# Fox/RetNet trunk on one core: ScalarE's reads of a transposed tile issued ahead of VectorE's

## The chip, the cores and the metric

The kernel runs on one core of a Trainium2 chip. The metric is the device time of one execution in microseconds (us). Five engines work side by side, each through its own instructions in the order in which they were issued: TensorE (PE in the profile; its weight loads are PEld), VectorE (DVE), ScalarE (ACT), GpSimd (POOL, here used to issue DMAs) and SyncE (SP, which issues the other DMAs). They wait for each other through semaphores.

## The reference

Two layers over x (1, 512, 2048), each with its own token mixer, and a LayerNorm behind each.

```python
def reference(x, ...):
    h = x
    for i in range(2):
        y = fox_branch(...) if i % 2 == 0 else retention_branch(...)
        h = layer_norm(DEEPNORM_ALPHA * h + y, ln_gain[i], ln_bias[i])
    return h

def fox_branch(x, w_in, b_f, q_gain, k_gain, w_out):     # 16 heads of 128
    q, k, v, gate, f_logit = split(x @ w_in)
    q = rms_norm(heads(q), q_gain)                       # over each head's 128
    k = rms_norm(heads(k), k_gain)
    c = cumsum(log_sigmoid(f_logit + b_f))
    s = q @ k.T * 128 ** -0.5 + c[:, None] - c[None, :]  # causal
    o = softmax(s) @ v
    return (o * silu(gate)) @ w_out

def layer_norm(x, g, b):
    return (x - mean(x)) * rsqrt(var(x) + 1e-5) * g + b
```

The second layer (`retention_branch`) projects the first layer's output into queries, keys, values and gates of 8 heads, applies a rotary turn, a decaying causal product, a group norm, the gate and an output projection.

## The kernel before, in words

**Products in three parts.** Every fp32 operand is split into a high part (`h`, rounded to the matmul's format; a ScalarE copy, L325) and a low part (`l` = value minus `h`; a VectorE subtraction, L326). `mm3` makes one product of three matmuls (L330 to L332). For a block of weights the parts are `w_h` and `w_l`, in rings of three buffers, of 128 x 1024 elements each.

**Blocks in a fixed order.** The projections are cut into blocks of weights of 512 KB: `w_raw` and `w_q` are the loaded weights, `acc` the accumulators in PSUM. Many units use a scheme of seven products instead of eight, whose weights are sums (VectorE, L595) and whose activations are sums too (forms "a" and "s"). A block of the wide kind is 12 matmuls of 512 columns.

**A planner at build time.** The class `Order` writes down, slot by slot, the order in which each engine gets its work. A slot splits the weights of the block two ahead, multiplies one block, and then lets the waiting tasks take one step each. Tasks are Python generators; each `yield need(...)` names what the step costs by the planner's own estimate, and which buffers it takes. The planner changes nothing at run time: the engines go through what was written. The order between engines is then put in as waits by the tile framework, which looks at what each instruction reads and writes, in the order in which the program issues them.

**Two small PSUM buffers.** `mmp` is a ring of two buffers of 128 x 512 fp32, one PSUM bank each. Transposes, scores and other small products go through them, between the blocks.

**Queries and keys of the first layer.** For each of 8 pairs of heads, the task `Pair.normed` scales the raw queries and keys (L1093), and for each of four pieces of 128 positions transposes them on TensorE into an `mmp` buffer `t`: columns 0 and 1 are the two heads' queries, 2 and 3 their keys. `to_parts` then reads `t` and writes the high part to the tile `qk_h` (ScalarE, L1102, with the gain as scale) and the low part to the tile `qk_l` (VectorE, L1103, which reads `t` and the high part), first for the queries and then for the keys. That makes 32 calls, and 64 instructions on each engine. In pairs 6 and 7 (`quick`, transposes at L1112; others at L1122) the four pieces follow each other closely. The scores in `head` read `qk_h` and `qk_l`.

**The first layer's end.** The task `to_columns(m)` normalises 256 rows `z` and turns them into columns, the second layer's input. In 8 turns per `m` it transposes four 128 x 128 pieces of `z` into an `mmp` buffer (L1567); one turn later, four instructions read that buffer, multiply by the gain and add the bias, each for one column `j`, into the tile `raw` (named `aq` in the program): VectorE takes `j == 1` (L1583), ScalarE the other three (L1585). That is 16 instructions on VectorE and 48 on ScalarE. With `m == 0`, one turn later, `split_form` splits the piece into high and low part (`a`, L325 and L326). Between the turns the blocks' own splits (`w_h`, `w_l`) go through the same two engines.

Of the kernel before, what the change touches and what calls it, by code (L numbers as in the profile page):

```python
# [14 lines left out]
AF = mybir.ActivationFunctionType  # L15
ALU = mybir.AluOpType

P = 128
# [227 lines left out]
def need(dve=0.0, act=0.0, pe=0.0, wait=1, until=lambda: True, **rings):  # L246
    return dict(dve=dve, act=act, pe=pe, wait=wait, until=until, rings=rings)
# [3 lines left out]
def trunk(ctx: ExitStack, tc: tile.TileContext, xq, x, fb_f, columns, wf_in, narrow, wide, ln_g, ln_b, rot, decay,  # L251
          out):
    nc = tc.nc
# [7 lines left out]
    def f32(t):  # L261
        return t.bitcast(F32)
# [34 lines left out]
    gq, gk = cols[:, 0:1], cols[:, 1:2]  # L297
# [6 lines left out]
    def rsqrt_steps(dst, src, n, scale, eps, steps=True):  # L304

        h = pool.tile([P, n], F32, name="rsq_h", tag=f"rsq_h{n}")
        t = pool.tile([P, n], F32, name="rsq_t", tag=f"rsq_t{n}")

        nc.vector.tensor_scalar(h, src, 0.5 * scale, 0.5 * eps, op0=ALU.mult, op1=ALU.add)
        nc.vector.tensor_scalar(t.bitcast(I32), h.bitcast(I32), 1, None, op0=ALU.logical_shift_right)  # L310
        nc.vector.tensor_scalar(dst.bitcast(I32), t.bitcast(I32), -1.0, float(0x5EF759DF - 2 ** 31),
                                op0=ALU.mult, op1=ALU.add)
        for i in range(3):
            if i == 1 and steps:
                yield need(dve=1.2, wait=0)
            if n == 1:
                nc.vector.scalar_tensor_tensor(t, dst, h, dst, op0=ALU.mult, op1=ALU.mult)
            else:
                nc.vector.tensor_mul(t, dst, dst)
                nc.vector.tensor_mul(t, t, h)  # L320
            nc.vector.scalar_tensor_tensor(dst, t, 1.5, dst, op0=ALU.subtract, op1=ALU.mult)
# [670 lines left out]
    class Pair:  # L992
# [88 lines left out]
        def normed(self):  # L1081

            yield need(until=lambda: self.have == 4 and fox["norms"] == self.i)
            raw = [self.raw[s // 2][:, s % 2] for s in range(ST)]
            r = self.ss
            yield need(dve=1.2)
            yield from rsqrt_steps(*[r.rearrange("p a b -> p (a b)")] * 2, 4 * ST, 1.0 / P, QK_EPS)
            scaled = {}
            for s in range(ST):
                yield need(dve=0.6, wait=0)  # L1090
                scaled[s] = o.due
                v = raw[s].rearrange("p (h d) -> p h d", h=4)
                nc.vector.tensor_mul(v, v, r[:, s, :, None].to_broadcast([P, 4, P]))  # L1093
            yield need(until=lambda: all(free[t] for t in self.tags))
            for t in self.tags:
                take(t)
            self.qk = sb8("qk_h", self.tags[0], F32R), sb8("qk_l", self.tags[1], F32R)

            def to_parts(t, s):
                for i, gain in ((0, gq), (2, gk)):  # L1100
                    h, l = (p[:, i:i + 2, s * P:(s + 1) * P] for p in self.qk)
                    nc.scalar.activation(h, t[:, i:i + 2], AF.Copy, scale=gain)  # L1102
                    nc.vector.scalar_tensor_tensor(l, t[:, i:i + 2], gain, f32(h), op0=ALU.mult, op1=ALU.subtract)  # L1103
                self.due = o.due
                give("mmp")

            t, s, last = {}, ST if self.quick else 0, None
            for q in range(ST if self.quick else 0):
                yield need(act=0.75, dve=0.7, pe=0.45, wait=1 - q % 2, mmp=1, until=lambda: o.soon(scaled[q]))
                t[q] = by4(mmp())  # L1110
                for h in range(4):
                    nc.tensor.transpose(t[q][:, h], raw[q][:, h * P:(h + 1) * P], ident)  # L1112
                to_parts(t[q], q)
            can = lambda: s < ST and free["mmp"] and o.soon(scaled[s])
            while s < ST or last is not None:
                yield need(act=0.75, dve=0.7, pe=0.45, until=lambda: last is not None or can())
                new = None
                if can():
                    new = s
                    t[s] = by4(mmp())  # L1120
                    for h in range(4):
                        nc.tensor.transpose(t[s][:, h], raw[s][:, h * P:(h + 1) * P], ident)  # L1122
                    s += 1
                if last is not None:
                    to_parts(t[last], last)
                last = new
            give("in0")
            give("in1")
            fox["emptied"] = self.i + 1
            yield need()  # L1130
            fox["norms"] = self.i + 1
# [396 lines left out]
    def to_columns(m):  # L1528
        yield need(dve=2.6, until=lambda: quarters[2 * m] == quarters[2 * m + 1] == 4)
        quarters[2 * m] = quarters[2 * m + 1] = 0  # L1530
        mv, r = ln_factors(2 * m, 2 * m + 1)
        nb = pool.tile([P, 2], F32, name="ln_nb", tag="ln_nb", bufs=2)
        nc.vector.scalar_tensor_tensor(nb, mv[:, :, 0], -1.0, r, op0=ALU.mult, op1=ALU.mult)
        due = {}
        for e in range(2):
            yield need(dve=0.81, act=0.97)
            due[2 * m + e] = o.due
            for u in range(2):
                s = 2 * m + e
                z = z_part(s, u)  # L1540
                if u:
                    nc.scalar.activation(z, z, AF.Identity, scale=r[:, e:e + 1], bias=nb[:, e:e + 1])
                else:
                    nc.vector.tensor_scalar(z, z, mv[:, e, 0:1], r[:, e:e + 1], op0=ALU.subtract, op1=ALU.mult)
                nc.gpsimd.dma_start(z_norm[s][:, u * 1024:(u + 1) * 1024], z)
        if m == 0:
            new_quarters(0)
            new_form("a11")
            new_form("a12")
        else:  # L1550
            yield need(g0=1, g2=1)
            new_quarters(1)

        turns = [(2 * m + e, c) for c in ((0, 1, 2, 3) if m == 0 else (0, 2, 1, 3)) for e in range(2)]
        ps, i, last, made = {}, 0, None, []
        can = lambda: i < 8 and free["mmp"] and o.soon(due[turns[i][0]])
        while i < 8 or last is not None or made:
            yield need(dve=(0 if last is None else 0.35) + 0.6 * len(made), act=(0 if last is None else 0.9) + 0.5 * len(made),
                       pe=0.45, until=lambda: last is not None or made or can())
            new = None  # L1560
            if can():
                new = i
                s, c = turns[i]
                zs = z_part(s, c // 2)[:, c % 2 * 512:(c % 2 + 1) * 512]
                ps[i] = by4(mmp())
                for j in range(4):
                    nc.tensor.transpose(ps[i][:, j], zs[:, j * P:(j + 1) * P], ident)  # L1567
                i += 1
            for j in made:
                s, c = turns[j]  # L1570
                es = slice(s % 2 * P, (s % 2 + 1) * P)
                k = c % 2 * 4
                split_form(f"a1{c // 2 + 1}", aq[f"1{c // 2 + 1}"][:, k:k + 4, es], k, k + 4, es, s % 2 == 1)
            made = []
            if last is not None:
                s, c = turns[last]
                es = slice(s % 2 * P, (s % 2 + 1) * P)
                d = aq[f"{m + 1}{c // 2 + 1}"][:, c % 2 * 4:c % 2 * 4 + 4, es]
                for j in range(4):
                    k = c * 4 + j  # L1580
                    g, b = cols[:, 2 + k:3 + k], cols[:, 2 + KT + k:3 + KT + k]
                    if j == 1:
                        nc.vector.tensor_scalar(d[:, j], ps[last][:, j], g, b, op0=ALU.mult, op1=ALU.add)  # L1583
                    else:
                        nc.scalar.activation(d[:, j], ps[last][:, j], AF.Identity, scale=g, bias=b)  # L1585
                give("mmp")
                if m == 0:
                    made.append(last)
                elif s % 2:
                    there.add((f"2{c // 2 + 1}", c % 2))  # L1590
            last = new
        for u in range(2):
            for t in z_tags(u, m):
                give(t, 2)
            for key in ((u, m), (u, 2 * m), (u, 2 * m + 1)) if (u, m) == (1, 1) else ((u, m),):
                zt.pop(key, None)
# [435 lines left out]
```

## Time and profile before

| | |
|---|---|
| median of 3 runs | 2371.23 us (2368.53 to 2372.38) |
| profiled execution, own time | 2373.73 us |
| its span, first to last instruction | 2372.0 us |
| mean granted TensorE clock | 0.993 |
| busy: PE, DVE, ACT, POOL | 97%, 80%, 51%, 7% |
| high parts L1102 on ScalarE | 64 of 469 ns mean, first at 144.0, last at 798.1 us |
| low parts L1103 on VectorE | 64 of 481 ns mean, first at 146.5, last at 798.6 us |
| columns L1585 on ScalarE | 48 of 452 ns mean, first at 936.2, last at 1022.0 us |
| columns L1583 on VectorE | 16 of 405 ns mean, first at 937.4, last at 1021.2 us |

How to read the profile's lines: a row of the timeline gives start, length, engine, line, operation, `out<-in`, and in brackets the idle time of the engine just before it and what ended that. "x2" merges neighbours. Rows of waits give who waited for whom. In the table of windows each engine's busy time in that stretch is followed by the granted clock (1.00 is full speed) and the share of the DMA engines.

### The profile page before, as it was taken

What the parts mean: (1) busy time and instruction counts of PE and PEld (TensorE: products, weight loads), DVE (VectorE), ACT (ScalarE), POOL (GpSimd) and SP (SyncE); (2) the same over time, 40 slices, a digit from 0 to 9 for tenths busy, and PEclk for the clock granted to TensorE, in tenths of its full rate; (3) what the DMA queues carried; (4) which work ended last, traced back from release to release, by engine and by line L of the source; (5) the groups of instructions that cost most, each with busy time, mean ns of one, the idle gap of its engine ahead of it and who ended that gap; (6) DMA issues with size and microseconds to landing.
All of it is one profiled execution on the core that took longest, in us unless ns stands there. A gap on an engine that the chain in (4) does not pass through costs nothing.

```text
span 2372.0 us, 32919 instructions
## 1 busy us (share of the span) xinstructions
PE 2307.9 (97%) x12424; PEld 1975.0 (83%) x12424; DVE 1892.5 (80%) x2477; ACT 1213.4 (51%) x1762; POOL 165.7 (7%) x256
## 2 busy tenths in 40 slices
PE   9999999999999999999999999999999999999995
PEld 9878778879899778888889898988888898787784
DVE  5887787787765656689889888888988889987877
ACT  4546556556555534565444545354545445554533
POOL 0000000000000000010100101010101000011002
PEclk9999999999999999999999999999999999999998
DMA  6356455455544456684685857575756659679778
GB/s 225 123 199 198 160 187 187 154 181 184 195 151 155 139 199 241 225 186 157 207 263 211 249 174 222 197 203 186 218 186 209 204 171 274 209 256 295 234 247 190
DMA packets 186350, 477.36 MB, mean 201 GB/s; under 512 B 18224, under 2 KB 63424, under 8 KB 185680
## 3 DMA queue, kind: packets, MB, share of 16 engines
q1 hardware_dynamic: 160288, 399.48, 50.3%
q0 software_dynamic: 25904, 75.78, 12.7%
q8 instruction: 97, 1.59, 0.3%
q14 instruction: 61, 0.50, 0.1%
HBM read 415.39 MB, written 64.00 MB: 202 GB/s over the span
## 4 chain that ended last, share of the span: by engine, by line
PE 62%; DVE 7%; DMA 4%; issue 3%; ACT 3%; POOL 0%; SPq 0%; DVEq 0%; ACTq 0%; POOLq 0%
PE acc L330 19%; PE acc L331 19%; PE acc L332 19%; DVE w_l L326 3%; DMA w_raw<-in_wide 2%; ACT w_h L325 2%; PE mmp L331 1%; PE mmp L330 1%; PE mmp L332 1%; PE mmp L1303 1%; DVE w_q L595 1%; DMA room<-in_wide 1%; PE mmp L1835 1%; PE mmp L1155 0%; DVE z L1936 0%
## 5 line engine op out<-in xcount | busy, mean ns | idle before, releaser
L325 ACT ACTIVATE w_h<-w_q 128x1024 fp32r<-128x1024 f32 x360 | 380.6, 1059 | 417.9 <-DVE w_q L595 221.6
L326 DVE TENSOR_TENSOR w_l<-w_raw,w_h 128x1024 fp32r<-128x1024 f32 x314 | 383.5, 1222 | 201.8 <-ACT w_h L325 200.5
L330 PE MATMUL acc<-w_h,a 128*128 128x512 f32 (+1 forms) x1440 | 536.5, 373 | 7.2 <-DVE kept L488 4.6
L331 PE MATMUL acc<-w_l,a 128*128 128x512 f32 (+1 forms) x1440 | 529.4, 368 | 3.1 <-DVE w_l L326 2.9
L332 PE MATMUL acc<-w_h,a 128*128 128x512 f32 (+1 forms) x1440 | 528.9, 367 | 0.0
L325 ACT ACTIVATE w_h<-w_raw 128x1024 fp32r<-128x1024 f32 x314 | 331.7, 1058 | 374.5 <-PE acc L332 181.0
L326 DVE TENSOR_TENSOR w_l<-w_q,w_h 128x1024 fp32r<-128x1024 f32 x360 | 439.2, 1221 | 100.3 <-ACT w_h L325 96.7
L331 PE MATMUL acc<-w_l,s 128*128 128x512 f32 (+1 forms) x1280 | 488.4, 382 | 10.7 <-DVE w_l L326 10.7
L330 PE MATMUL acc<-w_h,s 128*128 128x512 f32 (+1 forms) x1280 | 492.2, 385 | 1.6 <-ACT w_h L325 1.6
L332 PE MATMUL acc<-w_h,s 128*128 128x512 f32 (+1 forms) x1280 | 486.9, 380 | 0.0
L330 PEld LDWEIGHTS acc<-w_h,a 128*128 128x128 f32 x1440 | 272.5, 189 | 54.1 <-issue 8.5
L331 PEld LDWEIGHTS acc<-w_l,a 128*128 128x128 f32 x1440 | 272.8, 189 | 48.6 <-DVE w_l L326 7.5
L332 PEld LDWEIGHTS acc<-w_h,a 128*128 128x128 f32 x1440 | 272.3, 189 | 45.2
L331 PEld LDWEIGHTS acc<-w_l,s 128*128 128x128 f32 x1280 | 241.9, 189 | 60.0 <-DVE w_l L326 17.6
L332 PEld LDWEIGHTS acc<-w_h,s 128*128 128x128 f32 x1280 | 241.6, 189 | 45.8
L330 PEld LDWEIGHTS acc<-w_h,s 128*128 128x128 f32 x1280 | 241.6, 189 | 45.0 <-ACT w_h L325 2.0
L595 DVE TENSOR_TENSOR w_q<-w_q,w_raw 128x1024 f32<-128x1024 f32 x216 | 263.3, 1220 | 12.1 <-DMA w_raw<-in_wide 9.7
L332 PE MATMUL acc<-a,w_l 128*128 128x256 f32 x464 | 132.2, 285 | 1.7 <-DVE w_l L326 1.7
L330 PE MATMUL acc<-a,w_h 128*128 128x256 f32 x464 | 132.3, 285 | 1.5 <-ACT w_h L325 1.5
L331 PE MATMUL acc<-a,w_h 128*128 128x256 f32 x464 | 132.0, 285 | 0.0
L332 PE MATMUL acc<-s,w_l 128*128 128x256 f32 x448 | 126.8, 283 | 0.0
L331 PE MATMUL acc<-s,w_h 128*128 128x256 f32 x448 | 126.7, 283 | 0.0
(235 smaller groups left out, 2972.2 us busy)
## 6 DMA issues: line engine op xcount, KB each, us to landing
w_raw<-in_wide SPq DMA_DIRECT2D x364, 512.0 KB, 4.1
w_raw<-in_narrow SPq DMA_DIRECT2D x104, 512.0 KB, 3.7
w_q<-in_wide SPq DMA_DIRECT2D x72, 512.0 KB, 4.4
room<-in_wide SPq DMA_DIRECT2D x48, 512.0 KB, 4.5
y_s<-ny POOLq DMA_DIRECT2D x48, 256.0 KB, 7.1
y_s<-y POOLq DMA_DIRECT2D x40, 256.0 KB, 6.7
w_q<-in_narrow SPq DMA_DIRECT2D x18, 512.0 KB, 3.9
room<-in_narrow SPq DMA_DIRECT2D x18, 512.0 KB, 3.9
```

The source lines that it names most:

```text
L325: nc.scalar.activation(h, src, AF.Copy)
L326: nc.vector.tensor_sub(l, src, f32(h))
L330: nc.tensor.matmul(ps, a[0], b[0], start=start, stop=False, skip_group_check=True)
L331: nc.tensor.matmul(ps, a[0], b[1], start=False, stop=False, skip_group_check=True)
L332: nc.tensor.matmul(ps, a[1], b[0], start=False, stop=stop, skip_group_check=True)
L595: nc.vector.tensor_add(u.chain[c], u.chain[c], t)
L1303: nc.tensor.matmul(ps[:, k * P:], vh[:, k], pT[:, k, k * P:], start=k == 0, stop=k == ST - 1)
L1835: nc.tensor.transpose(ps[t - 1][:, i], g[t - 1][:, i * P:(i + 1) * P], ident)
```

## The change

In `to_parts` both high parts are issued first and then both low parts. In `to_columns` ScalarE's three columns (0, 2, 3) are issued first and VectorE's column 1 last. The instructions, their operands and their number are the same.

```diff
             def to_parts(t, s):
-                for i, gain in ((0, gq), (2, gk)):
-                    h, l = (p[:, i:i + 2, s * P:(s + 1) * P] for p in self.qk)
-                    nc.scalar.activation(h, t[:, i:i + 2], AF.Copy, scale=gain)
-                    nc.vector.scalar_tensor_tensor(l, t[:, i:i + 2], gain, f32(h), op0=ALU.mult, op1=ALU.subtract)
+
+                parts = [(gain, t[:, i:i + 2], *(p[:, i:i + 2, s * P:(s + 1) * P] for p in self.qk))
+                         for i, gain in ((0, gq), (2, gk))]
+                for gain, x, h, _ in parts:
+                    nc.scalar.activation(h, x, AF.Copy, scale=gain)
+                for gain, x, h, l in parts:
+                    nc.vector.scalar_tensor_tensor(l, x, gain, f32(h), op0=ALU.mult, op1=ALU.subtract)
                 self.due = o.due
                 give("mmp")
...
                 d = aq[f"{m + 1}{c // 2 + 1}"][:, c % 2 * 4:c % 2 * 4 + 4, es]
-                for j in range(4):
+                for j in (0, 2, 3, 1):
                     k = c * 4 + j
```

## The prediction

> **What bounds the kernel now.** I read the page's busy times first, then the windows by stage, then who waited for whom, and last the timeline of each stage that the change touches.
>
> ```profile
> span 2372.0 us, 32919 instructions
> PE 2307.9 (97%) x12424; PEld 1975.0 (83%) x12424; DVE 1892.5 (80%) x2477; ACT 1213.4 (51%) x1762; POOL 165.7 (7%) x256
> ```
>
> TensorE (PE) is the bound: 64.1 us of the span are not busy. An edit that leaves the matmuls alone can only give back some of these 64, and time in which the clock is down. So the question is which of TensorE's idle stretches end on the two waits that the diff touches. The windows (span of the window, busy us of PE, PEld, DVE, ACT, POOL, granted clock, DMA share, GB/s):
>
> ```profile
> 163.00:173.00 10.00, 8.32 (x36) 6.23 (x35) 9.34 (x13) 5.69 (x7) 0.53 (x1) 1.00 0.55 195
> 793.00:799.00 6.00, 3.79 (x18) 2.76 (x17) 3.91 (x8) 3.50 (x7) 0.00 (x0) 1.00 0.26 87
> 935.00:971.00 36.00, 32.92 (x159) 25.97 (x158) 19.69 (x28) 23.39 (x43) 0.25 (x1) 1.00 0.54 196
> 989.00:1026.40 37.40, 34.06 (x185) 27.29 (x184) 17.67 (x21) 23.96 (x40) 3.49 (x4) 1.00 0.80 236
> 1026.00:1100.00 74.00, 74.00 (x416) 65.04 (x417) 69.69 (x66) 43.06 (x46) 6.90 (x8) 1.00 0.73 199
> 967.80:971.20 3.40, 1.43 (x9) 0.96 (x8) 1.91 (x3) 3.40 (x6) 0.00 (x0) 1.00 0.22 83
> 971.20:974.60 3.40, 3.40 (x18) 3.40 (x17) 3.40 (x5) 0.43 (x1) 0.00 (x0) 0.50 0.47 158
> ```
>
> PE idles 1.68 and 2.21 us in two places of the first layer's query and key work, 3.08 and 3.34 us at the layer's end (935 to 971, 989 to 1026), and not at all in the 74 us behind. The last two rows: a stretch busy for 1.43 of 3.40 us, then one at clock 0.50, which costs 1.70 us more.
>
> **What the change removes.** No instruction is added, dropped or moved on its own engine: ScalarE (ACT) still issues both high parts, or three columns, in that order, and VectorE (DVE) its low parts and its one column. DMA issues and every queue keep their order too. Only the order between the two engines changes, so only waits do. The waits of today, in us in total, times, and the longest:
>
> ```profile
> ACT qk_h L1102 <- DVE qk_l L1103: 49.3, 32, 3.4
> DVE qk_l L1103 <- ACT qk_h L1102: 27.7, 36, 5.2
> PE mmp L330 <- ACT qk_h L1102: 0.9, 2, 0.5
> ACT raw L1585 <- DVE raw L1583: 22.4, 16, 2.7
> ```
>
> ScalarE's second high part (32 of 64) waits for VectorE's first low part though it needs nothing of it; VectorE then waits back for that high part. At the layer's end ScalarE's column 2 waits in all 16 turns for VectorE's column 1. What is shared is the transposed tile in PSUM: both engines read it. The first of the quick pairs (from pair 6 on), first ScalarE:
>
> ```profile
> 727.49 0.47 ACT L1102 ACTIVATE qk_h<-mmp,cols 128x256 fp32r<-128x256 f32 x1 [9.25 <-PE mmp L1112]
> 728.51 0.84 ACT L1102 ACTIVATE qk_h<-mmp,cols 128x256 fp32r<-128x256 f32 x2 [0.55 <-DVE qk_l L1103]
> ```
>
> and VectorE:
>
> ```profile
> 727.99 0.48 DVE L1103 SCALAR_TENSOR_TENSOR qk_l<-mmp,cols,qk_h 128x256 fp32r<-128x256 f32 x1 [5.20 <-ACT qk_h L1102]
> 729.02 0.88 DVE L1103 SCALAR_TENSOR_TENSOR qk_l<-mmp,cols,qk_h 128x256 fp32r<-128x256 f32 x2 [0.54 <-ACT qk_h L1102]
> ```
>
> Strict turns: high, low, high, low. Two in a row on one engine take 0.84 or 0.88, not 0.95: a pitch near 0.37 and 0.40. The "x2" at 728.51 is the keys' high part of one tile and, with no wait, the queries' of the next tile: the order is imposed inside a tile, not on all of qk_h. After the change both high parts end 0.84 after the start, then both low parts take 0.88: 1.75 with one handover, against 2.01 (727.49 to 729.50) now.
>
> A new wait: VectorE's first low part will stand behind both high parts, up to 0.37 us later than now. Where VectorE arrives late (28 of 32 tiles: of its 36 waits 32 are the 0.54 before a second low part, 17.3 of the 27.7 us) both are long done and it costs nothing; where it is early (4 tiles) it loses 0.37 and saves 0.54 plus the 0.08 of the closer pitch. Its last low part, for which alone the scores and the next transposes wait, always ends earlier, by 0.25 to 0.62. What is queued behind on VectorE (low parts of weights, w_l) gains with it. The Trainium skill, PSUM — Partial Sum Buffer, section "PSUM bank collisions raise a hardware error", says that any two engines on one bank must be kept apart, reads against reads included; by that the first low part has to wait for both high parts, as I charge it. Were it free to start after the first one, 4 x 0.37 = 1.5 us of VectorE time would not be lost, of which 0.4 lies on PE's path. The strict turns above agree with the rule.
>
> **Term 1, weights behind the parts (163 to 173).**
>
> ```profile
> 158.35 0.48 DVE L1103 SCALAR_TENSOR_TENSOR qk_l<-mmp,cols,qk_h 128x256 fp32r<-128x256 f32 x1 [0.83 <-ACT qk_h L1102]
> 159.38 0.48 DVE L1103 SCALAR_TENSOR_TENSOR qk_l<-mmp,cols,qk_h 128x256 fp32r<-128x256 f32 x1 [0.54 <-ACT qk_h L1102]
> 160.32 1.23 DVE L326 TENSOR_TENSOR w_l<-w_q,w_h 128x1024 fp32r<-128x1024 f32 x1 [0.46 <-ACT w_h L325]
> 165.30 0.50 PE L331 MATMUL acc<-w_l,s 128*128 128x512 f32 x1 [0.67 <-DVE w_l L326]
> 172.04 0.50 PE L331 MATMUL acc<-w_l,s 128*128 128x512 f32 x1 [1.00 <-DVE w_l L326]
> ```
>
> PE's 0.67 and 1.00 us end on w_l, and VectorE is 93% busy. A tile's parts cost it 0.54 + 0.46 of waiting (the 0.46 because ScalarE's w_h is behind the held high part). Two tiles, this one and the one before it, come ahead of the first stall and give up to 2 x 1.0, which I cut to 1.5 for the early arrival here; a third, between the stalls, gives 0.54 more. 1.5 covers 0.67; 1.5 + 0.54 - 0.67 = 1.4 covers 1.00. I take 1.7 of 1.68 idle, bounds 0 and 1.7.
>
> **Term 2, the quick pairs (793 to 799, and the one before).**
>
> ```profile
> 790.49 0.47 ACT L1102 ACTIVATE qk_h<-mmp,cols 128x256 fp32r<-128x256 f32 x1 [0.55 <-DVE qk_l L1103]
> 793.60 0.47 ACT L1102 ACTIVATE qk_h<-mmp,cols 128x256 fp32r<-128x256 f32 x1 [1.32 <-DVE qk_l L1103]
> 791.95 1.22 DVE L326 TENSOR_TENSOR a<-y_raw,a 128x1024 fp32r<-128x1024 f32 x1 [0.46 <-ACT a L325]
> 794.11 0.48 DVE L1103 SCALAR_TENSOR_TENSOR qk_l<-mmp,cols,qk_h 128x256 fp32r<-128x256 f32 x1 [0.54 <-ACT qk_h L1102]
> 794.74 0.63 PE L1112 MATMUL mmp<-ident,qk_raw 128*128 128x128 f32 x4 [1.69 <-DVE qk_l L1103]
> ```
>
> PE's fourth transposes want the buffer that the low part ending at 794.59 frees. New: the first tile's high parts end 0.65 earlier than 790.96, so ScalarE's a and then VectorE's (791.95) move 0.65 forward, to about 791.3 to 792.5; the two low parts then run to 793.3, with no held high part between. That is 1.3 before 794.59, leaving 0.4 of the 1.69. The rest of the 2.21 (0.52: the scores, which wait for qk_h twice, 0.9 us in all, for a last high part held by the turns) goes: 1.8. The other of the two, 0.9 - 0.5 = 0.4 at the pair before, goes likewise. Sum 2.2, bounds 0.5 and 2.7.
>
> **Term 3, the layer's end.** One turn on ScalarE,
>
> ```profile
> 950.27 0.81 ACT L1585 ACTIVATE raw<-mmp,cols 128x128 f32<-128x128 f32 x2 [1.35 <-DVE raw L1583]
> 950.97 1.05 ACT L325 ACTIVATE w_h<-w_raw 128x1024 fp32r<-128x1024 f32 x1
> 952.44 0.45 ACT L1585 ACTIVATE raw<-mmp,cols 128x128 f32<-128x128 f32 x1
> 954.24 0.81 ACT L1585 ACTIVATE raw<-mmp,cols 128x128 f32<-128x128 f32 x2 [1.35 <-DVE raw L1583]
> ```
>
> on VectorE,
>
> ```profile
> 952.05 1.23 DVE L326 TENSOR_TENSOR w_l<-w_raw,w_h 128x1024 fp32r<-128x1024 f32 x1 [1.82 <-ACT w_h L325]
> 953.80 0.41 DVE L1583 TENSOR_SCALAR raw<-mmp,cols 128x128 f32<-128x128 f32 x1
> ```
>
> (the group of that column over the whole span, busy us, mean ns, idle before:)
>
> ```profile
> L1583 DVE TENSOR_SCALAR raw<-mmp,cols 128x128 f32<-128x128 f32 x16 | 6.5, 405 | 0.0
> ```
>
> and PE:
>
> ```profile
> 955.10 0.66 PE L1567 MATMUL mmp<-ident,z 128*128 128x128 f32 x4 [0.55 <-ACT raw L1585]
> 955.82 0.39 PE L331 MATMUL acc<-w_l,a 128*128 128x512 f32 x1
> 956.05 0.40 PE L332 MATMUL acc<-w_h,a 128*128 128x512 f32 x1
> ```
>
> This is a ring: w_h, VectorE's w_l (needs w_h), the split of a between, column 1, ScalarE's columns 2 and 3 (held 1.35), next w_h. It turns in 954.24 - 950.27 = 3.97 us. PE wants less: 955.82 - 955.10 for four transposes and a matmul, and 11 more matmuls (12 in a block) at 0.23: 3.25. So PE loses its lead and stalls, on transposes (buffer not yet read) and then on w_h and w_l.
>
> New: ScalarE's turn is 952.44 - 950.97 for w_h and a, and three columns at 0.36 (two take 0.81, one 0.45): 2.55. VectorE's is 953.80 - 952.05 and 0.41: 2.16. Both fit in 3.25, so PE is late for nothing. VectorE's column now stands behind three ScalarE columns; it comes at 953.80, and three columns from 952.44 would end at 953.61 (0.45 + 2 x 0.36): no wait, with 0.19 to spare, less a handover of 0.03 (727.96 to 727.99). The buffer comes free after column 1 at 954.20, not after column 3 at 955.05. Of the idle 3.08 + 3.34 = 6.4 I take 6.0: the second half is also fed by loads at DMA share 0.80. The halved clock behind 967.8 to 971.2 goes with its idle: 1.7. The Trainium skill, TensorE: Matmul & The Clock Gate, Part 1, has the clock halved after a window with little activity; the two rows agree, and the 1.7 stands on the rows. Sum 7.7, bounds 3.0 (first half alone) and 8.1.
>
> **Sum.** 1.7 + 2.2 + 7.7 = 11.6 us. Behind each term PE is the bound again or the same lateness goes on from an earlier start, so it should last. Profiled execution: 2373.73 (1.73 outside its span), to 2362.1. The median of the runs shown is 2.50 lower: 2371.23 - 11.6 = **2359.6**.
>
> **Rivals.** *Given back to loads.* The chain of waits (start, length, what) has in the second half:
>
> ```profile
> 986.90 8.51 DMA w_raw<-in_wide
> 995.51 1.07 ACT w_h L325
> ```
>
> ```profile
> 999.46 0.47 PE L330 MATMUL acc<-w_h,a 128*128 128x512 f32 x1
> ```
>
> That w_h and a w_l of 1.23 behind it are ready near 997.8, 1.6 ahead of PE's block at 999.46, the one I take to use them. If the landing doesn't move with PE, PE comes 3.08 + 1.7 = 4.8 earlier and stalls 3.2. If term 1's is eaten by loads likewise, 11.6 - 3.2 - 1.7 = 6.7; with term 2 lost too, 4.5: 2364.5 to 2367. Against it: the buffer it fills is freed by a w_l that follows PE. *Nothing changes.* A held high part only swaps places with a held low part and PE's stalls end on something else just behind: 2371. For it: PE idles only 10.7 us in the places named. *Slower.* VectorE's column at the layer's end waits for ScalarE's three. The margin is 0.16 us; if ScalarE falls 0.86 behind, VectorE loses 0.7 a turn, 11.2 in 16 turns, all of it on w_l and so on PE, term 3 falls away, and 2371.2 - 3.9 + 11.2 = 2378.5. It decides when the loss passes 3.9/16 = 0.24 a turn. Against: VectorE idles 0.0 before this column now, always behind a w_l that itself needs ScalarE.
>
> **Chances.** Forecast (gain 8 to 16) 0.61; given back 0.23 (half of it beyond 0.2%); no change 0.10; slower 0.06. A measurement tells about 0.2%, 4.7 us. Faster 0.73, same 0.21, slower 0.06. Lower end: all bounds (1.7 + 2.7 + 8.1), 2 us more from small delays of PE that show as no idle time, 2 us of spread between runs: 2354. Upper end, between given back (2367) and no change (2371): 2369.
>
> **What would show it.** The wait of qk_h on qk_l gone (49.3 to under 5) and of raw on raw (22.4 to 0); qk_l's on qk_h 27.7 to about 12; ring pitch 3.97 to 3.25; PE idle under 1 us in each of the two layer-end stretches, and the 0.50 clock behind the first gone. The prediction is wrong if w_h waits for loads instead at 995 and PE idles there, or if column 1 shows idle time before it.

## The result, and the profile after

| | before | after |
|---|---|---|
| median of 3 runs | 2371.23 us (2368.53 to 2372.38) | 2348.45 us (2348.23 to 2351.51) |
| profiled execution, own time | 2373.73 us | 2351.51 us |

The ratio is 0.991 (0.9888 to 0.9933): 22.8 us by the medians, 22.2 by the profiled executions. The forecast was 11.6, with 17.2 at its lower end. The time went the way that was predicted, and about twice as far.

The page of the changed kernel opens with span and busy times:

```profile
span 2349.7 us, 32939 instructions
PE 2299.9 (98%) x12424; PEld 1974.7 (84%) x12424; DVE 1890.6 (80%) x2477; ACT 1211.3 (52%) x1762; POOL 165.7 (7%) x256
```

TensorE's time that is not busy fell from 64.1 to 49.8 us, by 14.3. The span fell by 22.3. The other 8.0 us left TensorE's *busy* time (2307.9 to 2299.9), with the same 12424 matmuls and the same mean granted clock, 0.993. That is the first hint of what the prediction missed.

The lines of the two files shift by 2 or 3: high parts are L1104, low parts L1106, the quick pairs' transposes L1115, the layer end's transposes L1570, its columns L1586 (VectorE) and L1588 (ScalarE). The waits of the changed kernel (total, times, longest):

```profile
ACT qk_h L1104 <- PE mmp L1115: 15.3, 5, 9.2
DVE qk_l L1106 <- ACT qk_h L1104: 12.6, 5, 5.6
PE mmp L1115 <- DVE qk_l L1106: 0.4, 1, 0.4
```

The 49.3 us of `qk_h` on `qk_l` and the 22.4 us of `raw` on `raw` have no row any more. `qk_l` on `qk_h` fell from 27.7 to 12.6. The windows that answer to those of before (weights behind the parts, the layer's two ends, and the stretch where the clock was halved; columns as there):

```profile
158.00:173.00 15.00, 15.00 (x68) 12.22 (x67) 13.59 (x19) 8.02 (x11) 0.53 (x1) 1.00 0.40 140
926.00:960.00 34.00, 34.00 (x172) 28.30 (x171) 23.67 (x32) 24.56 (x44) 1.06 (x2) 1.00 0.67 240
976.00:1008.60 32.60, 32.60 (x190) 28.38 (x189) 20.61 (x24) 25.38 (x42) 3.49 (x4) 1.00 0.94 284
957.00:963.00 6.00, 6.00 (x45) 5.69 (x44) 4.99 (x7) 2.38 (x3) 0.00 (x0) 1.00 0.65 214
```

TensorE has no idle time in any of them, and the clock is full. The ring at the layer's end, ScalarE's and VectorE's rows of one and a half turns:

```profile
945.38 1.14 ACT L1588 ACTIVATE raw<-mmp,cols 128x128 f32<-128x128 f32 x3
947.09 1.06 ACT L325 ACTIVATE w_h<-w_raw 128x1024 fp32r<-128x1024 f32 x1 [0.57 <-PE acc L332]
948.57 1.14 ACT L1588 ACTIVATE raw<-mmp,cols 128x128 f32<-128x128 f32 x3
```

```profile
946.73 0.41 DVE L1586 TENSOR_SCALAR raw<-mmp,cols 128x128 f32<-128x128 f32 x1
949.92 0.40 DVE L1586 TENSOR_SCALAR raw<-mmp,cols 128x128 f32<-128x128 f32 x1
```

The three columns stand in one piece ("x3"), VectorE's column shows no idle time before it, and `w_h` now waits for TensorE: TensorE sets the pace. The pitch is 948.57 - 945.38 = 3.19 us, against 3.97.

**Where the time went.** Both kernels issue the same matmuls in the same order, so the two traces can be laid beside each other, matmul for matmul. The *lead* of a matmul is its start in the trace of before minus its start in the other trace. Where the lead grows, time was won. For every kernel of this study (the edits follow in the next section), at the times of before:

| lead at us | 100 | 200 | 700 | 800 | 900 | 1000 | 1050 | 2100 | 2300 |
|---|---|---|---|---|---|---|---|---|---|
| changed kernel | -1.98 | 0.80 | 3.85 | 7.33 | 7.32 | 13.28 | 18.48 | 18.22 | 22.40 |
| the same again (e6) | -1.91 | 0.28 | 4.20 | 7.64 | 7.62 | 13.59 | 18.78 | 19.03 | 21.49 |
| parts only (e1) | 0.09 | 2.60 | 5.95 | 9.41 | 9.38 | 9.36 | 10.14 | 10.34 | 14.27 |
| columns only (e2) | 0.47 | 0.53 | 1.49 | 1.51 | 1.47 | 7.43 | 12.63 | 13.93 | 17.09 |
| columns 0, 2, 1, 3 (e3) | 0.28 | 0.28 | 0.25 | 0.29 | 0.29 | 3.43 | 5.81 | 6.62 | 9.40 |
| columns 1, 0, 2, 3 (e4) | -0.23 | -0.26 | -0.02 | 0.02 | -0.01 | -2.71 | -4.84 | -3.71 | 0.23 |
| before again (e5) | -0.29 | -0.76 | 0.57 | 0.62 | 0.63 | 0.65 | 0.62 | 0.32 | 2.66 |
| quick pairs only (e7) | 0.48 | 0.56 | 0.48 | 3.95 | 3.93 | 3.84 | 4.61 | 4.52 | 5.62 |
| all columns on ScalarE (e8) | -0.35 | 2.39 | 5.65 | 9.13 | 9.15 | 15.12 | 20.31 | 21.99 | 23.52 |

In the changed kernel the two places of term 1 gave 2.2 us (0.96 at 165.30, 1.24 at 172.04; another 0.5 was won just ahead of them, from 155 to 162), the pairs between 300 and 660 gave 3.1 (at 328, 342, 494, 505, 514 and 603 us), the quick pairs 3.5, and the layer's end 11.2 (7.32 to 18.48): 20.0 against 11.6. Before 100 us 2.0 were lost, and behind 2100 some 4 won; no instruction that the change touches is issued in either place.

### The profile page after: what moved, and what is told of

Same layout as the page of the kernel before. It is cut to its first block, busy times and chain, and to the rows that moved or that the text cites. A ratio compares the mean times of both kernels' runs of the same rounds, so it can differ in the third digit from the quotient of the medians.

```text
span 2349.7 us, 32939 instructions
## 1 busy us (share of the span) xinstructions
PE 2299.9 (98%) x12424; PEld 1974.7 (84%) x12424; DVE 1890.6 (80%) x2477; ACT 1211.3 (52%) x1762; POOL 165.7 (7%) x256
## 4 chain that ended last, share of the span: by engine, by line
PE 80%; DVE 9%; DMA 5%; ACT 3%; issue 3%; POOL 0%; SPq 0%; DVEq 0%; ACTq 0%; POOLq 0%
PE acc L331 24%; PE acc L330 24%; PE acc L332 24%; DVE w_l L326 3%; PE mmp L332 2%; PE mmp L331 2%; PE mmp L330 2%; ACT w_h L325 2%; PE mmp L1306 1%; DMA w_raw<-in_wide 1%; DVE w_q L595 1%; DMA v_sum<-in_wide 1%; DMA y_raw<-y_s 1%; PE mmp L1158 1%; DMA room<-in_wide 1%
```

## The experiments

Theory: everything that was won comes from the two orders, each in its own place, and the terms were right in place but counted too small, since TensorE's *idle time* was summed where its *lateness* counts. Rivals: parts and columns work on each other, or the rest of the gain lies in work far from the change.

**e1, the parts alone** (the first part of the diff; the columns stay as before).

> Only the first half of the change: both high parts ahead of both low parts; the layer's end as before. Theory: the gain follows TensorE's lateness, start to start, not its idle time. Between the two traces 9.3 us arise from 100 to 800 us (2.3 at the weights near 165, 3.5 at the quick pairs, 3.1 in pairs between, where transposes of the gates or of raw queries wait for a buffer that a low part frees). So 2371 - 9 = 2362 (2360.5 to 2364.5), TensorE's lateness at the layer's end unchanged (about 12 us). Rival: the 3.1 of the pairs between is chance, the prediction's terms 1 and 2 (3.9) or at most 6 are all: 2365 to 2367.

Measured: 2359.02 us (2358.47 to 2360.23), ratio 0.9948 (0.993 to 0.9966) to before on the same chip (2369.3). That is 1.5 us under the range that was given; of the 14.3 that its trace wins by 2300 us, 3.9 lie behind 2100. The lead grows by 9.3 us from 100 to 800, of which 3.4 lie between 200 and 700, where the prediction had charged nothing; at the layer's end 0.8. There the columns wait as before:

```profile
ACT raw L1588 <- DVE raw L1586: 22.4, 16, 2.7
```

**e2, the columns alone** (the second part of the diff).

> Only the second half of the change: ScalarE's three columns ahead of VectorE's; high and low parts in turns as before. Theory: 11.2 us at the layer's end, 2371 - 11 = 2360 (2357.5 to 2361.5), and the traces agree to 1.5 us up to 900 us. Rival: the further 4 us that the changed kernel won after 2100 us belong to the change (an earlier start meets the loads better): 2356 or less, and then e1 and this one together give more than 23. If the prediction's 7.7 was right, 2363.5.

Measured: 2361.11 us (2357.53 to 2363.8), ratio 0.9957 (0.994 to 0.9973). The lead grows by 11.16 us from 900 to 1050, to the hundredth what it grows by in the changed kernel, and by 0.1 from 100 to 200, where e1 won 2.5. The medians of e1 and e2 together give 18.5 us, not the rival's 23. This kernel arrives at the layer's end at nearly the time of before, so the same windows can be read:

```profile
935.00:971.00 36.00, 36.00 (x199) 30.87 (x198) 26.93 (x38) 24.46 (x44) 0.00 (x0) 1.00 0.65 232
989.00:1026.40 37.40, 37.40 (x228) 33.19 (x227) 29.15 (x32) 28.56 (x43) 3.49 (x4) 1.00 0.84 232
```

Look at the counts. In 36 us TensorE does 199 matmuls where it did 159, though its busy time rose only from 32.92 to 36.00, by 9%. (Some of the 40 are small ones that follow the stretch.) The two parts add up in the traces: 9.3 (e1, 100 to 800) and 11.2 (e2, 900 to 1050) make 20.5, and the changed kernel has 18.48 + 1.98 = 20.5 from 100 to 1050. So neither part of the change leans on the other.

**e3, one column of ScalarE's behind VectorE's** (the parts as before):

```diff
-                for j in range(4):
+                for j in (0, 2, 1, 3):
```

> Columns in the order 0, 2, 1, 3: one ScalarE column behind VectorE's instead of two; parts in turns as before. Theory of the ring (next weights' high part held by the columns behind VectorE's): the turn is 3.97 - 0.35 = 3.6 us in the first half, still over TensorE's 3.2, and 3.0 in the second, under it. So some stalls stay in the first half and none in the second: 8 to 10 of the 11 us, 2361 to 2363. Rival: what counts is when the small buffer comes free, which is only 0.35 earlier than before: half the gain, 2365 to 2367.

Measured: 2365.49 us (2364.33 to 2367.89), ratio 0.9979 (0.9969 to 0.9988). The layer's end (900 to 1050) gives 5.5 us, half of 11.2. The theory's size (8 to 10 us) missed, and the time is the one that the rival gave. VectorE's rows of this kernel give the pitch in the first half:

```profile
949.29 0.41 DVE L1583 TENSOR_SCALAR raw<-mmp,cols 128x128 f32<-128x128 f32 x1
952.92 0.41 DVE L1583 TENSOR_SCALAR raw<-mmp,cols 128x128 f32<-128x128 f32 x1
```

3.63 us, halfway between 3.97 and TensorE's 3.2: half of the loss a turn is left there. Yet the rival, by which only the buffer counts, does not have the place right: of the 5.6 us that e3 loses against e2, start to start, 1.2 stand at the transposes, which wait for the buffer, and 4.4 at `w_h` and `w_l`. What the theory had wrong is the second half. Four of its seven turns take 3.02 there, under TensorE's 3.2, but the others take 3.50, 4.30 and 5.02, and 2.8 us are lost.

**e4, VectorE's column ahead of all of ScalarE's** (the parts as before):

```diff
-                for j in range(4):
+                for j in (1, 0, 2, 3):
```

> Columns in the order 1, 0, 2, 3: all three ScalarE columns behind VectorE's; parts in turns as before. Theory of the ring: turn 4.3 us in the first half and 3.7 in the second, 0.35 more than before on each of 16 turns, of which all count once TensorE has lost its lead: slower by 4 to 6 us, 2375 to 2377. Rival of the buffer: it comes free 0.35 later, which shows only in the three stalls on transposes: slower by 1, 2372.

Measured: 2376.35 us (2372.95 to 2379.0), ratio 1.0024 (1.0013 to 1.0034). The layer's end is 4.8 us slower. ScalarE's rows:

```profile
947.20 1.16 ACT L1585 ACTIVATE raw<-mmp,cols 128x128 f32<-128x128 f32 x3 [1.70 <-DVE raw L1583]
951.52 1.16 ACT L1585 ACTIVATE raw<-mmp,cols 128x128 f32<-128x128 f32 x3 [1.70 <-DVE raw L1583]
```

All three columns wait, 1.70 us a turn, and the pitch is 4.32. The number of ScalarE's columns that stand behind VectorE's is 0, 1, 2, 3 in e2, e3, before and e4, and the layer's end gives +11.2, +5.5, 0 and -4.8 us: some 5.3 us for each column, or 0.33 a turn in 16 turns. The turn grows by as much as a further column of ScalarE's takes (0.35 to 0.36): for 1, 2 and 3 columns the steady turns take 3.63, 3.97 and 4.32 in the first half, and 3.02, 3.37 and 3.72 in the second. TensorE's transposes now wait for the buffer in several turns, as here:

```profile
952.74 0.66 PE L1567 MATMUL mmp<-ident,z 128*128 128x128 f32 x4 [0.92 <-ACT raw L1585]
```

Of the 16.0 us that e4 loses against e2, 8.2 stand at the transposes and the rest at `w_h` and `w_l`. So the place of the columns is the cause, and it acts in both ways: through the buffer and through the next weights. How the loss divides between the two was not tried by an edit of its own.

**e5, the kernel before once more**, to see what two traces of one program differ by.

> The kernel before, unchanged, for a second trace of it. Theory: the stalls at 2160 to 2168 us in the first trace (weights landing late, and a halved clock behind), 3.1 to 4.1 us that all four kernels of the first series lack, the slower one too, are chance of that one execution: this trace lacks them as well, so that about 2369 is what the kernel before takes. Rival: they belong to it, and any shift of the work ahead of them removes them: they are there again, within 0.5 us.

Measured: 2370.45 us, beside 2370.33 for before on that chip. Between 200 and 2100 the leads move by up to 1.7. Behind 2100 they grow by 2.3 us, here with no edit at all. The windows of 2150 to 2180, first of before, then of e5:

```profile
2150.00:2180.00 30.00, 26.59 (x109) 21.06 (x108) 24.57 (x24) 12.55 (x13) 2.20 (x4) 0.94 1.01 317
```

```profile
2150.00:2180.00 30.00, 28.17 (x117) 22.83 (x116) 26.12 (x25) 13.35 (x13) 2.20 (x4) 0.94 1.05 337
```

DMA is full in both, and TensorE idles 3.4 us in the one and 1.8 in the other: this stretch ends on transfers and differs by itself. The stall shrank in the second trace, and did not vanish. In the other eight traces the lead behind 2100 grows by 1.1 to 4.2 us, whatever the edit: the changed kernel's 4.2 there can't be told from chance, since a second execution of before already differs from the first by 2.3.

**e6, the changed kernel once more.**

> The changed kernel, unchanged, with more rounds beside the kernel before on the same chip. Theory: the two parts add up, 9.3 + 11.2 = 20.5 us: 2369 to 2348.5 (2347 to 2350), ratio 0.9913. Rival: the sum of the medians of the two halves, 10.3 + 8.2 = 18.5, because both give TensorE's lead back to the same loads: 2351.

Measured: 2352.54 us (2347.45 to 2353.33), ratio 0.9917 (0.9904 to 0.9931), that is 19.7 us of 2370.3 (17.8 by the medians). The median lies above the theory's range, and the interval of the ratio holds the theory's 20.5 as well as the rival's 18.5, so the times don't decide between them. The traces do: the lead grows by 11.16 at the layer's end again, by 9.6 from 100 to 800, and is -1.91 at 100 again.

**e7, the new order of the parts in pairs 6 and 7 alone** (`if self.quick:` the new order, else the old one; the columns as before).

> High parts ahead of low parts in pairs 6 and 7 alone, the six other pairs in turns, columns as before. Against the trace of before, theory: no step up to 720 us, 3.5 us from 730 to 800 (0.7 + 0.4, 1.3, 0.7 + 0.4), nothing at the layer's end. The prediction's 2.2, which counted TensorE's idle time, would show as 2.2. Rival: the late pairs gain only because earlier ones did: under 2.

Measured: 2368.19 us in one run. The lead grows by 3.47 between 700 and 800 and by nothing ahead of that. The transposes of its quick pair, and the window of term 1:

```profile
791.90 0.63 PE L1120 MATMUL mmp<-ident,qk_raw 128*128 128x128 f32 x4 [0.40 <-DVE qk_l L1106]
```

```profile
163.00:173.00 10.00, 8.35 (x36) 6.23 (x35) 9.34 (x13) 5.15 (x7) 0.53 (x1) 1.00 0.60 209
```

The 1.69 of before is 0.40, as worked out. The 1.65 us of idle time of term 1 stay where the other pairs keep the old order, so those pairs are its cause.

**e8, the whole change, with VectorE's column given to ScalarE** (`if j == 1:` to `if j == 4:`; no column is left on VectorE).

> The changed kernel with all four columns on ScalarE, none on VectorE, so that nothing is handed over in a turn. Theory: once no ScalarE work stands behind a VectorE column, TensorE sets the pace; ScalarE's turn of 2.5 + 0.35 = 2.85 is still under TensorE's 3.2: equal to the changed kernel within 1 us. Rival: the turn counts in full because the stage starts late and has to catch up, so 16 x 0.35 = 5.6 slower; or VectorE, 0.41 freer in a turn, was the limit: 2 or more faster.

Measured: 2350.4 us (2345.94 to 2351.33), ratio 0.991 (0.9897 to 0.9924). The layer's end gives 11.16 once more. ScalarE takes on 16 instructions and VectorE drops them:

```profile
PE 2299.3 (98%) x12424; PEld 1974.3 (84%) x12424; DVE 1885.6 (80%) x2461; ACT 1216.4 (52%) x1778; POOL 165.7 (7%) x256
```

TensorE paces that stretch already, so where the column runs is worth nothing more. e8's median lies 2.1 us under e6's, inside the spread of either; its trace does not lose the 1.9 us at the start. It is not shown to beat the changed kernel.

## Why the prediction was right in place and too small in size

**The waits and the ring: right.** Gone are the waits that were to go; 12 was given for `qk_l` on `qk_h` and 12.6 came; 3.25 for the ring's pitch and 3.19 came; TensorE's idle time in both stretches is 0. VectorE's column, which was to have 0.19 us to spare, waits for nothing. Where ScalarE has to catch up (its `w_h` waits 1.73 and 1.71 us for loads that land at 931.7 and 936.1), its turns take 2.5, near the 2.55 that was worked out for them, so TensorE loses nothing by those waits.

**What the first low part waits for: right.** In the first of the quick pairs, where VectorE is early:

```profile
723.64 1.57 ACT L1104 ACTIVATE qk_h<-mmp,cols 128x256 fp32r<-128x256 f32 x4 [9.20 <-PE mmp L1115]
```

```profile
724.51 1.66 DVE L1106 SCALAR_TENSOR_TENSOR qk_l<-mmp,cols,qk_h 128x256 fp32r<-128x256 f32 x4 [5.57 <-ACT qk_h L1104]
```

724.51 - 723.64 = 0.87 is two high parts (0.84) and a handover (0.03), not one: the first low part waits for both. ScalarE goes on with the other buffer's high parts meanwhile, without a gap ("x4"). That agrees with the Trainium skill, PSUM — Partial Sum Buffer, section "PSUM bank collisions raise a hardware error": any two engines must be kept apart on one bank, reads included, and two banks are free of each other.

**The halved clock: its 1.7 us are not shown.** The prediction let the halved clock behind 967.8 to 971.2 go with its idle time. In the changed kernel, which does not idle there, the clock is 1.00 (957 to 963). But e5, the same program as before, idles just as long in the same place, and its clock stays full behind it:

```profile
967.80:971.20 3.40, 1.41 (x9) 0.96 (x8) 1.91 (x3) 3.40 (x6) 0.00 (x0) 1.00 0.24 94
971.20:974.60 3.40, 3.40 (x29) 3.28 (x28) 3.40 (x5) 1.28 (x2) 0.00 (x0) 1.00 0.54 163
```

The Trainium skill, TensorE: Matmul & The Clock Gate, Part 1, puts the halved clock behind an idle window of about 3.4 us. Here the window ahead was busy for 1.43 us in before and for 1.41 in e5, with the halved clock behind the one and not behind the other, so that idle time alone does not settle it. Of the other traces that idle in this place, e1 and e7 have the halved clock and e3 and e4 don't. Nor did the full clock make e5's layer end shorter (its lead is 0.63 at 900 us and 0.62 at 1050): as much as the 1.5 us that it saved there was lost at longer waits ahead of it (0.59 at the transposes of 951.1) and behind it. The changed kernel wins 11.2 against either trace, with the halved clock or without.

**The size: the step that failed is "of the idle 3.08 + 3.34 = 6.4 I take 6.0", and the same step in each term.** TensorE's idle time was taken for what its stalls cost. Before, the scores of the pair ahead of term 2's show what that leaves out (start, length):

```profile
734.29 0.28 PE L332 MATMUL acc<-w_h,x 128*128 128x256 f32 x1
734.99 0.50 PE L330 MATMUL mmp<-qk_h 128*128 128x512 f32 x1 [0.42 <-ACT qk_h L1102]
735.51 0.51 PE L331 MATMUL mmp<-qk_l,qk_h 128*128 128x512 f32 x1
735.85 0.39 PE L332 MATMUL mmp<-qk_h,qk_l 128*128 128x512 f32 x1
736.08 0.28 PE L330 MATMUL acc<-w_h,a 128*128 128x256 f32 x1
```

and after:

```profile
730.37 0.28 PE L332 MATMUL acc<-w_h,x 128*128 128x256 f32 x1
730.49 0.40 PE L330 MATMUL mmp<-qk_h 128*128 128x512 f32 x1
730.72 0.40 PE L331 MATMUL mmp<-qk_l,qk_h 128*128 128x512 f32 x1
730.96 0.39 PE L332 MATMUL mmp<-qk_h,qk_l 128*128 128x512 f32 x1
731.18 0.28 PE L330 MATMUL acc<-w_h,a 128*128 128x256 f32 x1
```

From the first start to the last the same matmuls take 1.79 us and then 0.81: 0.98 lost, where the profile shows 0.42 idle. Matmuls overlap: in full flow one starts 0.23 us after the last and is busy for 0.40. A stall shows as idle only beyond that overlap: the first matmul of the scores could have started at 734.41 (0.12 behind 734.29, the pitch of its kind) and counts as idle only from 734.57, so 0.16 of its 0.58 don't show. The second matmul starts 0.52 behind the first instead of 0.23, so it lost 0.29 and shows no idle at all; the matmul behind lost another 0.11. Together with the clock, this is why busy time can fall with the work unchanged; the 8.0 us were not traced in full.

Term by term, forecast and measured: term 1 1.7 and 2.2 (its bound 1.7 was the idle time, and so no bound). Term 2 2.2 and 3.5, made of 0.4 and 1.1 at the pair before, 1.29 and 1.32 at the transposes, 0.52 and 1.1 at the scores behind. Only the transposes came out as given, since a stall was left standing there, with its own overlap in both traces. Term 3 7.7 and 11.2; its upper bound 8.1 was idle plus clock again. Counted from start to start, against the same matmuls in e2, the two stretches lose 4.4 and 5.3 us, 9.7 in all, where the profile shows 6.4 idle; with the 1.5 us of the halved clock that makes the 11.2. A nearer number could be had from the prediction's own rows (ring pitch 3.97, TensorE's want 3.25, 16 turns: 16 x 0.72 = 11.5), but that it comes so near is luck. The pitch of 3.97 is that of the first half alone. In the second, four of seven turns take 3.37 and the others 4.80, 4.65 and 5.37. The prediction's "2 us more from small delays of PE that show as no idle time" named the effect; it was 5.3 (20.0 - 11.6 - 3.1).

**A step left out: the pairs between 300 and 660 us, 3.1 us.** The prediction costed the parts only where a stall's row named `qk_l`, `qk_h` or `w_l`. Before, other stalls did not; two of them follow. The first, in e2 (old order of the parts) and then in e1 (new order):

```profile
326.81 0.63 PE L1314 MATMUL mmp<-ident,by_head 128*128 128x128 f32 x4 [0.69 <-PE acc L332]
```

```profile
325.56 0.63 PE L1317 MATMUL mmp<-ident,by_head 128*128 128x128 f32 x4
```

The row names TensorE itself, yet the wait goes with the order of the parts. In before the transposes start at 328.81, and VectorE's second low part, which frees the `mmp` buffer, ends at 328.70:

```profile
327.20 0.48 DVE L1103 SCALAR_TENSOR_TENSOR qk_l<-mmp,cols,qk_h 128x256 fp32r<-128x256 f32 x1
328.22 0.48 DVE L1103 SCALAR_TENSOR_TENSOR qk_l<-mmp,cols,qk_h 128x256 fp32r<-128x256 f32 x1 [0.54 <-ACT qk_h L1102]
```

The largest, 1.1 us at 505.85, names `sm`, the softmax's row; e2 and then e1:

```profile
504.35 2.42 PE L1303 MATMUL mmp<-pT,by_head 128*128 128x512 f32 x8 [1.50 <-DVE sm L1206]
```

```profile
500.98 2.20 PE L1306 MATMUL mmp<-pT,by_head 128*128 128x512 f32 x6 [0.38 <-DVE sm L1209]
```

VectorE in before has its last idle time ahead of that at 480.50, and then works 25 us without a gap:

```profile
480.50 1.23 DVE L590 TENSOR_TENSOR w_raw<-w_raw 128x1024 f32<-128x1024 f32 x1 [1.87 <-DMA w_raw<-in_wide]
```

In the changed kernel this instruction has a lead of 2.80, while TensorE's is 1.5: the load that it waits for came 1.3 earlier, relative to TensorE, and VectorE carried that to the softmax. That the order of the parts is the cause is shown by e1 and e2; that the load starts earlier because an earlier read frees its buffer is my reading, not tried by itself.

**The rivals.** *Given back to loads* did not happen: the second stretch, fed by loads, gave 5.2 of the 11.2 and has no idle time left. *Nothing changes* fell with it. *Slower* needed VectorE's column to wait for ScalarE's three; it does not, since it still arrives behind them. e4 shows only the reverse to be dear: ScalarE's columns held by VectorE's, with a turn of 4.32 us.

**Open.** The 2 us lost at the start and the 4 us won at the end (below). Whether the turns are imposed by the bank or by the tile was not tried. Why the clock halves behind the same idle time in one execution and not in another is open too.

## What to carry to other kernels

Where two engines read one buffer and are kept in strict turns, issue one engine's reads in one piece, first those of the engine whose next work closes the ring; each read of ScalarE's that no longer stood behind VectorE's shortened a turn by about its own length (0.35 us), and was worth 0.33 a turn where the ring paces TensorE. To cost a stall of a pipelined engine, compare starts with starts, matmul by matmul, since idle time leaves out the overlap of every stall and all of the short ones. A steady pitch times the number of turns will do only where all turns are alike. And look for stalls near the edit whose named releaser is the engine itself or a third tile: two of those hid 1.7 us here.

## What the runs showed of the hardware that was not expected

Both traces of the changed kernel lose 2 us near the start, with a halved clock that no other kernel shows there. The window 11 to 15, of before, of the changed kernel, and of e8:

```profile
11.00:15.00 4.00, 4.00 (x36) 4.00 (x35) 3.84 (x4) 3.19 (x3) 0.00 (x0) 1.00 1.04 420
```

```profile
11.00:15.00 4.00, 4.00 (x24) 4.00 (x23) 3.84 (x4) 3.34 (x4) 0.00 (x0) 0.57 1.01 405
```

```profile
11.00:15.00 4.00, 4.00 (x35) 4.00 (x35) 3.80 (x4) 3.33 (x4) 0.00 (x0) 1.00 1.01 397
```

24 matmuls instead of 36. Nothing that the change touches is issued before 144 us, and e8 holds the whole change and does not show it. So the new order by itself does not bring it; two traces against eight are too few to say whether it is chance.
